# The transpose of the meta tokens' probabilities moves behind the filler products

## The chip, the core and the metric

The kernel runs on one core of a Trainium2 chip. The core has TensorE (PE, which multiplies and transposes), VectorE (DVE), ScalarE (ACT), GpSimd (POOL) and SyncE (SP, which issues most DMAs). Each engine works through its own queue in the order in which it was written; between engines semaphores say when a tile is ready or free. TensorE writes to PSUM alone, from which VectorE and ScalarE fetch. The metric is device time of one execution in microseconds (us), lower is better.

## The reference

Two layers over 1024 tokens and 16 meta tokens put ahead of them, of width 1024. A layer norms its input and projects it to Fourier features, queries, keys, values and a gate; a Fourier half and an attention half are gated and projected back. The attention has four heads, and each is the difference of two softmax maps over all 1040 positions:

```python
s = jnp.einsum('bqhcd,bkhcd->bhcqk', qb, k).astype(jnp.float32) * scale
p = jax.nn.softmax(s, axis=-1)
a = p[:, :, 0] - lam_f * p[:, :, 1]
o = jnp.einsum('bhqk,bkhd->bqhd', a, vf)
```

## The kernel before

The attention of a layer goes head by head, in four groups of two query tiles of 128 rows (in the first layer the last group has a third tile, of the 16 meta tokens). The text numbers these tiles in the order of the program: 0 to 35 in the first layer, 36 to 67 in the second. A tile goes through these steps:

- `scores`: for each of the two maps six products into the one tile S of PSUM (L633, L635; the first map is "first scores", the second "second scores"). VectorE takes S out, negated and with its row maximum, into `p` in SBUF (L640, "the maximum"), ScalarE raises it (L643). The next scores can't start before the maximum has emptied S. Of the first map's `p` there are two buffers, of the second's one. L651 mixes the two maps into the first one's `p` ("the mix").
- `drain`, one tile later: `transposes` turns the mixed map in two batches of four 128x128 transposes (L661), each into a bank M of PSUM; ScalarE and VectorE fetch each batch as a high and a low part, `ath` (L666) and `atl` (L667). The ninth transpose, L669, turns the 16 columns of the meta tokens into a third bank ("m" in the prediction); two copies (L672) and a subtraction (L673) put it into `att`.
- at the end of a group, `values`: 24 products with `ath` and `atl` (L681) and one with `att` (L682), from which `osb` is copied (L684); `finish` transposes `osb` (L695, L697) and writes the gated result.

There are three banks M, and transposes of queries (L612), of keys (L585), values and `finish` take theirs from the same three. A bank that is asked for comes free with the last fetch out of an earlier one.

Between these steps the program calls `fill(n)`: a generator hands out the projections of the next heads (L545, into banks G, with the splitting of weights into `wh` and `wl`, L180 and L181, and the norm of `qk`, L501) and then the output projection of the Fourier half (L283). These are the fillers. They have low priority and are not to be issued before the instruction that stands `LAG` entries back in `marks`, a list to which `scores` and `transposes` append.

The order of each engine's queue is not that of the program text: a scheduler lays the instructions out by priority and by its own timeline, and decides which bank and buffer each tile gets.

```python
        def drain(item, pa):
            h, gi, i, t = item
            transposes(pa, i, t)
            fill(3)
```

Of the kernel before, what the change touches and what calls it, by code (L numbers as in the profile page):

```python
# [18 lines left out]
P = 128  # L19
DEPTH = 2  # L20
D = 1024
SEQ = 1024
NMETA = 16
L = SEQ + NMETA
# [24 lines left out]
def trunk(ctx: ExitStack, tc, x, meta, ngain, w_in, w_f, qg, kg, lq1, lk1, lq2, lk2, subg, w_out,  # L49
          ident_d, chan_d, rope_d, dft_d, dftt_d, out, dbg=None):  # L50
    nc = tc.nc
    pe, act, dve, pool, sp = nc.tensor, nc.scalar, nc.vector, nc.gpsimd, nc.sync
# [12 lines left out]
    def nm(s):  # L65
        uid[0] += 1
        return f"{s}_{uid[0]}"
# [4 lines left out]
    def bank():  # L72
        return psM.tile([P, 512], F32, tag="M", name=nm("M"))
# [4 lines left out]
    def f(ap):  # L78
        return ap.bitcast(F32)


    ident = cst.tile([P, P], F32, name="ident")
# [13 lines left out]
    def tile_rows(t):  # L96
        return NMETA if t == NT else P
# [456 lines left out]
    def attention(li, wk, store, fill, marks, ready, progress):  # L554
# [13 lines left out]
        def group_tiles(gi):  # L568
            return [2 * gi, 2 * gi + 1] + ([NT] if gi == 3 and li < DEPTH - 1 else [])
# [24 lines left out]
        def build_values(h):  # L594
            va = store[h][1]
            vh = wk.tile([P, NT, P], F32R, tag="vh", name=nm("vh"), bufs=1)
            vl = wk.tile([P, NT, P], F32R, tag="vl", name=nm("vl"), bufs=1)
            act.copy(vh, va[:, 0:NT])
            pool.tensor_tensor(vl, va[:, 0:NT], f(vh), op=ALU.subtract)
            vm = va[0:NMETA, NT, :]  # L600
            for o in (0, 32, 64):
                act.copy(vt[o:o + NMETA], vm)
            pool.tensor_tensor(vt[0:NMETA], vm, f(vt[0:NMETA]), op=ALU.subtract)
            return vh, vl
# [19 lines left out]
        def scores(keys, gq, i, t, ls, gaps):  # L624
            R = tile_rows(t)
            qo = P * i
            l2 = sm.tile([P, 1], F32, tag="l2", name=nm("l2"))
            pp = []
            for c in range(2):
                q, ql, kk = gq[0][c], gq[1][c], keys[c]  # L630
                ps = big()
                for a, b in CHUNKS:
                    pe.matmul(ps[0:R, C0 + a:C0 + b], lhsT=q[:, qo:qo + R], rhs=kk[:, a:b], start=True, stop=False)  # L633
                for a, b in CHUNKS:
                    ins = pe.matmul(ps[0:R, C0 + a:C0 + b], lhsT=ql[:, qo:qo + R], rhs=kk[:, a:b],  # L635
                                    start=False, stop=True)
                marks.append(ins.ins)
                mx = sm.tile([P, 1], F32, tag=f"mx{c}", name=nm("mx"))
                pc = wk.tile([P, L], F32, tag=f"p{c}", name=nm("p"), bufs=2 - c)
                dve.tensor_scalar(pc[0:R], ps[0:R, C0:C0 + L], -1.0, None, op0=ALU.mult, op1=ALU.min,  # L640
                                  accum_out=mx[0:R])
                lc = (ls[0:R, i:i + 1], l2[0:R])[c]
                act.activation(pc[0:R], pc[0:R], AF.Exp, bias=mx[0:R], scale=-1.0, accum_out=lc)  # L643
                pp.append(pc)
                gaps[c]()
            r2 = sm.tile([P, 1], F32, tag="r2", name=nm("r2"))
            dve.reciprocal(r2[0:R], l2[0:R])
            cc = sm.tile([P, 1], F32, tag="cc", name=nm("cc"))
            dve.scalar_tensor_tensor(cc[0:R], ls[0:R, i:i + 1], lamb[0:R, li:li + 1], r2[0:R],
                                     op0=ALU.mult, op1=ALU.mult)  # L650
            dve.scalar_tensor_tensor(pp[0][0:R], pp[1][0:R], cc[0:R], pp[0][0:R], op0=ALU.mult, op1=ALU.add)  # L651
            return pp[0]

        def transposes(pa, i, t):
            R = tile_rows(t)
            qo = P * i
            for c in range(2):
                pb = bank()
                for j in range(4):
                    kt = 4 * c + j  # L660
                    pe.transpose(pb[:, R * j:R * j + R], pa[0:R, P * kt:P * kt + P],  # L661
                                 ident[0:R, 0:R])
                src = pb[:, 0:4 * R].rearrange("p (j r) -> p j r", j=4)
                hi = ath[:, 4 * c:4 * c + 4, qo:qo + R]
                with tc.high_priority(EVAC):
                    act.copy(hi, src)  # L666
                    dve.tensor_tensor(atl[:, 4 * c:4 * c + 4, qo:qo + R], src, f(hi), op=ALU.subtract)  # L667
            pb = bank()
            ins = pe.transpose(pb[0:NMETA, 0:R], pa[0:R, SEQ:L], ident[0:R, 0:R])  # L669
            marks.append(ins.ins)  # L670
            for o in (0, 64):
                act.copy(att[o:o + NMETA, qo:qo + R], pb[0:NMETA, 0:R])  # L672
            dve.tensor_tensor(att[32:32 + NMETA, qo:qo + R], pb[0:NMETA, 0:R], f(att[0:NMETA, qo:qo + R]),  # L673
                              op=ALU.subtract)

        def values(vals, w):
            vh, vl = vals
            po = bank()
            for kt in range(NT):
                for i, (v, a) in enumerate(((vh, ath), (vh, atl), (vl, ath))):  # L680
                    pe.matmul(po[:, 0:w], lhsT=v[:, kt, :], rhs=a[:, kt, 0:w], start=kt == 0 and i == 0, stop=False)  # L681
            pe.matmul(po[:, 0:w], lhsT=vt, rhs=att[:, 0:w], start=False, stop=True)  # L682
            osb = wk.tile([P, 272], F32, tag="osb", name=nm("osb"), bufs=1)
            act.copy(osb[:, 0:w], po[:, 0:w])  # L684
            return osb
# [35 lines left out]
        def flush_finish():  # L721
            if fin[0] is not None:
                finish(*fin[0])
                fin[0] = None

        def drain(item, pa):
            h, gi, i, t = item
            transposes(pa, i, t)
            fill(3)
            tiles = group_tiles(gi)  # L730
            if i == len(tiles) - 1:
                flush_finish()
                osb = values(vals[h], sum(tile_rows(t) for t in tiles))
                fin[0] = (h, gi, osb, sums[h, gi])
                if gi == 3 and h + 1 < NH:
                    vals[h + 1] = build_values(h + 1)
# [7 lines left out]
        for n, item in enumerate(items):  # L744
            h, gi, i, t = item
            if i == 0:
                sums[h, gi] = sm.tile([P, 3], F32, tag="ls", name=nm("ls"))
            pa = scores(keys[h], queries[h, gi], i, t, sums[h, gi],
                        (lambda: (fill(2), flush_finish()), lambda: fill(2)))
            if i == 0 and gi < 3:  # L750
                queries[h, gi + 1] = build_queries(h, gi + 1)
            if gi == 0 and i == 0 and h > 0:
                fill(XHD[li])
            if pend is not None:
                drain(*pend)
            if h + 1 < NH and gi >= KEYS[li]:
                build_keys(h + 1, progress.get(h + 1, 0), 1)
            pend = (item, pa)
            fill(1)
            if gi == 3 and i == len(group_tiles(3)) - 2:  # L760
                yield h + 1
                if h + 1 < NH:
                    build_keys(h + 1, 3)
                    queries[h + 1, 0] = build_queries(h + 1, 0)
        fill(3)
        drain(*pend)
        flush_finish()

# [84 lines left out]
    with tc.tile_pool(name="in0", bufs=2, side="right", reuse_waits="tile") as wk:  # L853
        for t in list(range(MT)) + [NT] + list(range(MT, NT)):
            R = tile_rows(t)
# [9 lines left out]
    for li in range(DEPTH):  # L865
# [12 lines left out]
        marks, done, ready, nh, post = [], {0}, set(), {}, {}  # L878
# [17 lines left out]
        def fill(n):  # L896
            credit[0] += n * FILL[li]
            while credit[0] >= 1.0:
                credit[0] -= 1.0
                with ExitStack() as es:  # L900
                    es.enter_context(tc.high_priority(0))
                    if len(marks) >= LAG[li]:
                        es.enter_context(tc.issue_after(marks[-LAG[li]]))
                    if next(filler, False) is False:
                        return
# [95 lines left out]
```

## Time and profile before

| | us |
|---|---|
| median of 3 runs (1213.86 to 1215.79) | 1213.92 |
| the profiled execution | 1215.41 |
| its span in the trace | 1213.6 |
| TensorE busy | 1163.2 |
| VectorE busy | 833.5 |
| ScalarE busy | 675.9 |
| GpSimd busy | 148.5 |

The span is the time from the first to the last instruction that the trace shows; the time of the execution has a little around it. A row of waits says which engine, before which line, waited for which engine's line, how long in all, how often, and the longest. In a timeline the bracket at the end of a row is the idle time of the engine just before it and what ended it. The ends of matmuls are modelled, so that rows on TensorE overlap; the distance of two starts tells what one takes.

### The profile page before, as it was taken

To read this page: it belongs to the slowest core of one execution; us is meant where nothing else is said; L and a number is where in the kernel's file an instruction comes from. 1 tells how busy PE (TensorE), PEld (TensorE's weight loads), DVE (VectorE), ACT (ScalarE), POOL (GpSimd) and SP (SyncE) were. 2 spreads that over 40 slices of the span, in tenths; PEclk is the share of its full clock that TensorE was granted. 3 is DMA by queue.
4 is the path that set the end of the run, shared out by engine and by line. 5 is a ranking of instruction groups with operands and counts; after the bars stand their busy time and mean duration, and the time that the engine had idled before them with its cause. 6 is when DMAs were issued, how large, how long until landed. Compare 5 with 4: busy or idle time off the path is not lost.

```text
span 1213.6 us, 18701 instructions
## 1 busy us (share of the span) xinstructions
PE 1163.2 (96%) x6676; PEld 1001.6 (83%) x6676; DVE 833.5 (69%) x1803; ACT 675.9 (56%) x1644; POOL 148.5 (12%) x157
## 2 busy tenths in 40 slices
PE   6999999999999999999999999999999999999998
PEld 5999986877787787788879999877888888878786
DVE  6352546788788789888683525367787887987863
ACT  5332325677767667666453223356676776866740
POOL 1101023010211201100011000140111112101000
PEclk9999999999999998999999999999999999999899
DMA  7420303012012014744335202030120210473253
GB/s 236 134 70 18 91 28 101 7 31 77 14 47 61 14 32 148 221 150 131 134 127 167 70 19 90 29 100 8 43 58 23 57 49 20 143 220 128 101 159 117
DMA packets 103613, 105.46 MB, mean 87 GB/s; under 512 B 11233, under 2 KB 87585, under 8 KB 103265
## 3 DMA queue, kind: packets, MB, share of 16 engines
q1 hardware_dynamic: 103104, 99.59, 26.4%
q0 software_dynamic: 416, 4.70, 1.1%
q8 instruction: 52, 0.85, 0.3%
q14 instruction: 41, 0.33, 0.1%
HBM read 74.62 MB, written 29.62 MB: 86 GB/s over the span
## 4 chain that ended last, share of the span: by engine, by line
PE 80%; DVE 8%; ACT 6%; DMA 3%; issue 2%; POOL 1%; SPq 1%; ACTq 0%; DVEq 0%; POOLq 0%
PE G L545 23%; PE G L283 13%; PE G L349 8%; PE S L349 7%; PE M L681 7%; PE S L633 4%; PE S L635 4%; PE M L661 3%; PE S L545 3%; DVE p L640 2%; PE M L390 2%; ACT p L643 2%; DVE p L651 1%; DMA wst<-in_w_in_dram 1%; PE M L401 1%
## 5 line engine op out<-in xcount | busy, mean ns | idle before, releaser
L545 PE MATMUL G<-wh,hT 128*128 128x512 f32 x896 | 307.5, 400 | 2.8 <-ACT va L484 1.0
L545 PEld LDWEIGHTS G<-wh,hT 128*128 128x128 f32 x896 | 167.4, 188 | 42.9 <-ACT wh L180 1.9
L643 ACT ACTIVATE p<-p,mx 128x1040 f32<-128x1040 f32 x136 | 158.6, 1166 | 69.6 <-DVE p L640 68.4
L640 DVE TENSOR_SCALAR_CACHE_REDUCE p<-S 128x1040 f32<-128x1040 f32 x136 | 167.9, 1234 | 40.7 <-PE S L635 33.4
L545 PE MATMUL G<-wl,hT 128*128 128x512 f32 x448 | 176.4, 395 | 0.6 <-DVE wl L181 0.6
L283 PE MATMUL G<-wh,yh 128*128 128x512 f32 (+2 forms) x276 | 107.4, 402 | 6.5 <-ACT yh L789 4.0
L181 DVE TENSOR_TENSOR wl<-wst,wh 128x512 fp32r<-128x512 f32 x128 | 85.7, 701 | 29.5 <-ACT wh L180 29.2
L283 PE MATMUL G<-wl,yh 128*128 128x512 f32 (+2 forms) x276 | 105.8, 392 | 0.0
L180 ACT CAST wh<-wst 128x512 fp32r<-128x512 f32 x128 | 74.7, 620 | 52.5 <-DMA wst<-in_w_in_dram 23.5
L545 PEld LDWEIGHTS G<-wl,hT 128*128 128x128 f32 x448 | 84.3, 188 | 16.3 <-DVE wl L181 1.2
L349 PE MATMUL G<-hT,wh 128*128 128x384 f32 (+3 forms) x384 | 96.4, 331 | 0.0
L283 PE MATMUL G<-wh,yl 128*128 128x512 f32 (+1 forms) x260 | 93.0, 398 | 0.0
L499 POOL TENSOR_TENSOR rsq<-ss,nhalf 128x12 f32<-128x12 f32 x24 | 54.9, 2287 | 307.0 <-DVE ss L497 261.8
L349 PE MATMUL S<-hT,wh 128*128 128x256 f32 (+3 forms) x384 | 91.0, 321 | 1.4 <-DVE sg L437 1.3
L667 DVE TENSOR_TENSOR atl<-M,ath 128x512 fp32r<-128x512 f32 x136 | 86.2, 655 | 5.5 <-ACT ath L666 4.6
L651 DVE SCALAR_TENSOR_TENSOR p<-p,cc,p 128x1040 f32<-128x1040 f32 (+1 forms) x68 | 88.2, 1297 | 1.3
L635 PE MATMUL S<-k,ql 128*128 128x264 f32 (+3 forms) x408 | 88.1, 323 | 0.0
L666 ACT CAST ath<-M 128x512 fp32r<-128x512 f32 x136 | 72.7, 565 | 15.3 <-PE M L661 14.5
L661 PE MATMUL M<-ident,p 128*128 128x128 f32 x544 | 73.8, 271 | 0.1
L681 PE MATMUL M<-ath,vh 128*128 128x256 f32 (+1 forms) x256 | 73.4, 287 | 0.2 <-DVE atl L667 0.2
L681 PE MATMUL M<-ath,vl 128*128 128x256 f32 (+1 forms) x256 | 73.0, 285 | 0.0
L681 PE MATMUL M<-atl,vh 128*128 128x256 f32 (+1 forms) x256 | 72.8, 284 | 0.0
(193 smaller groups left out, 2408.1 us busy)
## 6 DMA issues: line engine op xcount, KB each, us to landing
wst<-in_w_in_dram SPq DMA_DIRECT2D x64, 192.0 KB, 2.8
xt<-in_x_dram SPq DMA_DIRECT2D x16, 512.0 KB, 3.9
wst<-in_w_in_dram SPq DMA_DIRECT2D x32, 256.0 KB, 4.5
wst<-in_w_out_dram SPq DMA_DIRECT2D x16, 512.0 KB, 4.3
xmid<-xt SPq DMA_DIRECT2D x16, 512.0 KB, 2.8
xt<-xmid SPq DMA_DIRECT2D x16, 512.0 KB, 4.6
tab<-in_dft_dram POOLq DMA_DIRECT2D x2, 2096.0 KB, 10.9
yfd<-sg SPq DMA_DIRECT2D x8, 520.0 KB, 2.7
```

The lines of the kernel that those rows point to most:

```text
L180: act.copy(h, self.staged[q][:, j, :])
L181: dve.tensor_tensor(l, self.staged[q][:, j, :], f(h), op=ALU.subtract)
L283: pe.matmul(pb[0:m, 0:e - c], lhsT=a[:, k, 0:m], rhs=b[2 * k + n][:, c:e], start=k == 0 and i == 0, stop=k == 3 and i == n_pass - 1)
L349: pe.matmul(o, lhsT=w[k][:, c:c + P], rhs=hT[:, k, s, a:b], start=k == 0 and i == 0, stop=k == KT - 1 and i == 2)
L545: pe.matmul(pss[t][0:part.shape[-1], a:b], lhsT=part, rhs=w[k][:, a:b], start=k == 0 and i == 0, stop=k == KT - 1 and i == len(pairs) - 1)
L635: ins = pe.matmul(ps[0:R, C0 + a:C0 + b], lhsT=ql[:, qo:qo + R], rhs=kk[:, a:b], start=False, stop=True)
L640: dve.tensor_scalar(pc[0:R], ps[0:R, C0:C0 + L], -1.0, None, op0=ALU.mult, op1=ALU.min, accum_out=mx[0:R])
L643: act.activation(pc[0:R], pc[0:R], AF.Exp, bias=mx[0:R], scale=-1.0, accum_out=lc)
L651: dve.scalar_tensor_tensor(pp[0][0:R], pp[1][0:R], cc[0:R], pp[0][0:R], op0=ALU.mult, op1=ALU.add)
L661: pe.transpose(pb[:, R * j:R * j + R], pa[0:R, P * kt:P * kt + P], ident[0:R, 0:R])
L667: dve.tensor_tensor(atl[:, 4 * c:4 * c + 4, qo:qo + R], src, f(hi), op=ALU.subtract)
L681: pe.matmul(po[:, 0:w], lhsT=v[:, kt, :], rhs=a[:, kt, 0:w], start=kt == 0 and i == 0, stop=False)
```

## The change

The ninth transpose with its three followers becomes a function of its own, and `drain` calls it behind `fill(3)` instead of ahead of it. The mark that `transposes` appends is now the last of the eight transposes, no longer the ninth.

```diff
--- before.py
+++ after.py
@@ -658,16 +658,19 @@
                 pb = bank()
                 for j in range(4):
                     kt = 4 * c + j
-                    pe.transpose(pb[:, R * j:R * j + R], pa[0:R, P * kt:P * kt + P],
-                                 ident[0:R, 0:R])
+                    ins = pe.transpose(pb[:, R * j:R * j + R], pa[0:R, P * kt:P * kt + P], ident[0:R, 0:R])
                 src = pb[:, 0:4 * R].rearrange("p (j r) -> p j r", j=4)
                 hi = ath[:, 4 * c:4 * c + 4, qo:qo + R]
                 with tc.high_priority(EVAC):
                     act.copy(hi, src)
                     dve.tensor_tensor(atl[:, 4 * c:4 * c + 4, qo:qo + R], src, f(hi), op=ALU.subtract)
+            marks.append(ins.ins)
+
+        def meta_transpose(pa, i, t):
+            R = tile_rows(t)
+            qo = P * i
             pb = bank()
-            ins = pe.transpose(pb[0:NMETA, 0:R], pa[0:R, SEQ:L], ident[0:R, 0:R])
-            marks.append(ins.ins)
+            pe.transpose(pb[0:NMETA, 0:R], pa[0:R, SEQ:L], ident[0:R, 0:R])
             for o in (0, 64):
                 act.copy(att[o:o + NMETA, qo:qo + R], pb[0:NMETA, 0:R])
             dve.tensor_tensor(att[32:32 + NMETA, qo:qo + R], pb[0:NMETA, 0:R], f(att[0:NMETA, qo:qo + R]),
@@ -727,6 +730,7 @@
             h, gi, i, t = item
             transposes(pa, i, t)
             fill(3)
+            meta_transpose(pa, i, t)
             tiles = group_tiles(gi)
             if i == len(tiles) - 1:
                 flush_finish()
```

What the scheduler makes of it differs in many places from the first drain on. The first place is the drain of tile 9, on TensorE. M_3341 is the ninth transpose, S_3397 further down the second scores of tile 11. Before, from the second batch of transposes on:

```order
L661 MATMUL M_3334<-ident,p_3121 128x128 x4
L669 MATMUL M_3341<-ident,p_3121 16x128
L545 MATMUL G_3553<-wh_2816,hT_150 128x512
L545 MATMUL G_3553<-wl_2817,hT_150 128x512
L545 MATMUL G_3553<-wh_2816,hT_150 128x512
L545 MATMUL G_3553<-wh_2820,hT_150 128x512
```

Fifteen more fillers follow there, then two transposes of queries, then the scores S_3397. After, the end of the fillers and what follows:

```order
L545 MATMUL G_3553<-wl_2840,hT_150 128x512
L545 MATMUL G_3553<-wh_2839,hT_150 128x512
L673 MATMUL M_3350<-ident,p_3121 16x128
L612 MATMUL M_3419<-ident,qk_2029 128x128 x2
L661 MATMUL M_3430<-ident,p_3250 128x128 x4
L633 MATMUL S_3397<-k_2604,qb_3167 128x264
L633 MATMUL S_3397<-k_2604,qb_3167 128x512
```

The 18 fillers now stand ahead of the ninth transpose (L673 after the change), and six transposes lie between it and the scores.

The second place is VectorE's queue at tiles 57 and 58. p_11323 is written by the mix of tile 57 (L651), p_11443 by the first maximum of tile 58 (L640). Before, from the reciprocal that precedes the mix to that maximum:

```order
L647 RECIPROCAL r_2085_11389<-l_2066_11314 128x1
L649 SCALAR_TENSOR_TENSOR cc_11391<-ls_11196,lamb,r_2085_11389 128x1
L651 SCALAR_TENSOR_TENSOR p_11323<-p_11360,cc_11391,p_11323 128x1040
L667 TENSOR_TENSOR atl<-M_11394,ath 128x4x128
L501 TENSOR_TENSOR qk_10641<-qk_10641,rsq_11628 128x768
L667 TENSOR_TENSOR atl<-M_11401,ath 128x4x128
L181 TENSOR_TENSOR wl_11505<-wst_11502,wh_11504 128x512
L181 TENSOR_TENSOR wl_11509<-wst_11502,wh_11508 128x512
L512 TENSOR_TENSOR r_2135_11631<-qk_10641,cgt 128x192
L513 TENSOR_TENSOR r_2136_11632<-qk_10641,sgt 128x12x8
L514 TENSOR_TENSOR r_2136_11632<-qk_10641,sgt 128x12x8
L640 TENSOR_SCALAR p_11443,mx_11442<-S_11435 128x1040
```

After, from that maximum on, in two pieces that follow each other; first the fetches, `qk` and the keys:

```order
L640 TENSOR_SCALAR p_11443,mx_11442<-S_11435 128x1040
L181 TENSOR_TENSOR wl_11499<-wst_11492,wh_11498 128x512
L666 TENSOR_TENSOR atl<-M_11401,ath 128x4x128
L676 TENSOR_TENSOR att<-M_11417,att 16x128
L647 RECIPROCAL r_2085_11389<-l_2066_11314 128x1
L708 TENSOR_SCALAR so_11340<-so_11340 128x2
L501 TENSOR_TENSOR qk_10641<-qk_10641,rsq_11628 128x768
```

and then up to the mix:

```order
L649 SCALAR_TENSOR_TENSOR cc_11391<-ls_11196,lamb,r_2085_11389 128x1
L589 SCALAR_TENSOR_TENSOR k_11080<-M_11422,kgc,k_11080 64x384
L181 TENSOR_TENSOR wl_11505<-wst_11502,wh_11504 128x512
L711 TENSOR_TENSOR rso_11345<-rso_11345,r_2072_11338 128x2
L512 TENSOR_TENSOR r_2135_11631<-qk_10641,cgt 128x192
L513 TENSOR_TENSOR r_2136_11632<-qk_10641,sgt 128x12x8
L651 SCALAR_TENSOR_TENSOR p_11323<-p_11360,cc_11391,p_11323 128x1040
```

The mix of tile 57 stood nine instructions ahead of the maximum and now stands thirteen behind it.

The third place is TensorE's queue at the same tiles after the change. M_11401 is the second batch of transposes of tile 56, M_11417 its ninth, S_11435 and S_11452 are the first and the second scores of tile 58, M_11422 holds keys:

```order
L661 MATMUL M_11401<-ident,p_11206 128x128 x4
L673 MATMUL M_11417<-ident,p_11206 16x128
L633 MATMUL S_11435<-k_10045,qa_11250 128x264
L633 MATMUL S_11435<-k_10045,qa_11250 128x512
L633 MATMUL S_11435<-k_10045,qa_11250 128x264
L635 MATMUL S_11435<-k_10045,ql_8650 128x264
L635 MATMUL S_11435<-k_10045,ql_8650 128x512
L635 MATMUL S_11435<-k_10045,ql_8650 128x264
L585 MATMUL M_11422<-ident,qk_10641 128x128 x3
L633 MATMUL S_11452<-k_10046,qb_11251 128x264
L633 MATMUL S_11452<-k_10046,qb_11251 128x512
```

Before, 18 fillers stood between the first scores and the ninth transpose of tile 56, and six more fillers, keys and the first batch of tile 57 (p_11323) between that and the second scores; now the ninth transpose stands ahead of the first scores, and keys alone between the two scores.

## Rows read from the trace of the kernel before

**Rows 1.** The page: busy time and share of the engines, granted clock by slice
```profile
PE 1163.2 (96%) x6676; PEld 1001.6 (83%) x6676; DVE 833.5 (69%) x1803; ACT 675.9 (56%) x1644; POOL 148.5 (12%) x157
...
PEclk9999999999999998999999999999999999999899
```

**Rows 2.** Waits of TensorE from 187 to 1176 us: engine, tile, line, releaser
```profile
PE M L669 <- DVE atl L667: 13.2, 10, 1.8
PE S L633 <- DVE p L640: 5.2, 6, 1.4
PE G L283 <- ACT yh L789: 4.0, 2, 2.7
...
PE M L695 <- ACT osb L684: 0.8, 1, 0.8
...
PE M L669 <- DVE ql L620: 0.5, 2, 0.3
...
PE M L669 <- ACT osb L697: 0.2, 1, 0.2
```

**Rows 3.** Timeline at tile 9, TensorE and VectorE (start, length, what)
```profile
321.39 0.65 PE L661 MATMUL M<-ident,p 128*128 128x128 f32 x4
...
322.78 1.28 DVE L667 TENSOR_TENSOR atl<-M,ath 128x512 fp32r<-128x512 f32 x2
...
323.51 0.28 PE L669 MATMUL M<-ident,p 128*16 128x128 f32 x1 [1.48 <-DVE atl L667]
```

**Rows 4.** Timeline between the two scores of tile 37
```profile
828.60 0.39 PE L545 MATMUL G<-wl,hT 128*128 128x512 f32 x1
828.83 0.40 PE L545 MATMUL G<-wh,hT 128*128 128x512 f32 x1
...
828.57 1.24 DVE L640 TENSOR_SCALAR_CACHE_REDUCE p<-S 128x1040 f32<-128x1040 f32 x1 [0.77 <-PE S L635]
...
829.87 0.75 PE L633 MATMUL S<-k,qb 128*128 128x264 f32 x3 [0.65 <-DVE p L640]
```

**Rows 5.** Timeline where m releases a maximum, TensorE and VectorE
```profile
870.51 0.27 PE L669 MATMUL M<-ident,p 128*16 128x128 f32 x1
...
870.82 1.24 DVE L640 TENSOR_SCALAR_CACHE_REDUCE p<-S 128x1040 f32<-128x1040 f32 x1 [1.46 <-PE M L669]
```

**Rows 6.** Timeline of TensorE ahead of the second scores of tile 57
```profile
1126.89 0.38 PE L612 MATMUL M<-ident,qk 128*128 128x128 f32 x2
1127.11 0.60 PE L661 MATMUL M<-ident,p 128*128 128x128 f32 x4
1127.47 0.72 PE L633 MATMUL S<-k,qb 128*128 128x264 f32 x3
...
1128.52 0.39 PE L283 MATMUL G<-wh,yl 128*128 128x512 f32 x1
```

**Rows 7.** VectorE's groups by line: busy us, mean ns, idle before
```profile
L651 DVE SCALAR_TENSOR_TENSOR p<-p,cc,p 128x1040 f32<-128x1040 f32 (+1 forms) x68 | 88.2, 1297 | 1.3
...
L667 DVE TENSOR_TENSOR atl<-M,ath 128x512 fp32r<-128x512 f32 x136 | 86.2, 655 | 5.5 <-ACT ath L666 4.6
L181 DVE TENSOR_TENSOR wl<-wst,wh 128x512 fp32r<-128x512 f32 x128 | 85.7, 701 | 29.5 <-ACT wh L180 29.2
...
L589 DVE SCALAR_TENSOR_TENSOR k<-M,kgc,k 64x384 fp32r<-64x384 f32 (+1 forms) x48 | 27.7, 577 | 16.2 <-ACT k L588 15.1
...
L501 DVE TENSOR_TENSOR qk<-qk,rsq 128x768 f32<-128x768 f32 x24 | 23.3, 972 | 6.0 <-POOL rsq L499 5.9
```

**Rows 8.** Stretches: busy time of each engine, granted clock (PEclk), DMA
```profile
253.00:256.00 3.00, 1.19 (x8) 0.80 (x7) 2.90 (x7) 2.17 (x7) 2.27 (x1) 1.00 0.29 85
...
470.00:476.00 6.00, 5.88 (x27) 5.84 (x28) 5.90 (x16) 4.14 (x11) 0.00 (x0) 0.51 0.99 312
...
1142.00:1148.00 6.00, 5.85 (x21) 5.17 (x22) 2.56 (x6) 3.95 (x11) 0.00 (x0) 0.50 0.00 0
```

**Rows 9.** The chain that ended last: 24 value products of a group
```profile
432.70 2.83 PE M L681 x24
```

## The prediction

> **What bounds the kernel now.** I read the page first: TensorE is busy for 1163.2 of 1213.6 us [rows 1], so the time changes by what is added to or taken from its 50 us of idle time, nearly nothing else. Next came the waits of TensorE between 187 and 1176 us, the two attention stretches with the ends of their layers [rows 2]. The transpose of the meta tokens' probabilities (L669, "m" below) waits 13.2 us for the vector engine's `atl` in 10 places, 0.5 us for `ql` and 0.2 us for a copy of `osb`: 13.9 us, over a quarter of all idle time. Second are the scores (S, L633), 5.2 us behind the maximum L640 that empties their only PSUM tile.
>
> The timeline at tile 9 shows what m waits for [rows 3]: its transposes start at 321.39, the pair of `atl` at 322.78, each about 0.65, and m starts at 323.51, when the first of the pair is done. The three M banks are then held, two by the tile's own transposes, and m gets the first that is emptied. All work behind m on TensorE waits, though the filler products there need nothing of it.
>
> **The change part by part.** No instruction is added or removed, on any engine; m still brings two copies on ScalarE and a subtraction on the vector engine, and no DMA. They feed the last value product alone, and the 24 value products ahead of it, 2.83 us [rows 9], hide them. The sum is made against the profiled execution, 1215.4 us around its span of 1213.6, which is 1.5 above the median of the runs, 1213.9.
>
> *Removed.* With the filler products between the transposes and m, a bank is free when m is reached: at tile 9, 18 of them at 0.23 us [rows 4] are 4.1 us, against the 1.48 waited. I take all of the 13.9 us as gone and count apart the places where m waits anew. -13.9.
>
> *The cover that is taken from the scores.* m is the last reader of `p`, which has two buffers, so the first maximum two tiles on can't write before m is done, and the second scores of that tile can't write S before this maximum is done. A maximum released by m alone starts 0.31 after m's start [rows 5] and takes 1.24; the scores follow a maximum's end by 0.06 (828.57 + 1.24 = 829.81, scores at 829.87 [rows 4]). So 1.61 us lie from m to the second scores. Before, the filler products stood there: 18 at tile 9. After, they stand ahead of m, and behind it are two transposes of queries and four of the next tile's probabilities, which took 0.58 from 1126.89 to 1127.47 [rows 6]; with 0.1 for m itself (a transpose's slot by the same rows), 1.61 - 0.68 = 0.93 us is waited. So little stands behind m at nine tiles (7, 9, 18, 27, 44, 46, 52, 60, 62): 8.4 us. At two (2, 11) three transposes of queries stand there, 0.1 more cover: 1.7. At six (13, 15, 16, 20, 25, 54) two or three filler products remain as well, and 0.2 to 0.5 is waited: 2.3. Together +12.4. That such a wait is real, the trace before has once: at 828.83 the last of only three filler products between two scores, then 0.65 of idle time [rows 4]. Behind the maximum that waits for m stand a gate, `att`, `ql` and the next tile's `atl`, which gives M banks back; nothing on TensorE asks for those before its second scores. The lower bound is 0, if something else on TensorE is late there anyway; the upper is a further 0.5 at each of the 17, for a vector engine still busy with other work when m ends, 8 us.
>
> *Two places where the vector engine's order turns.* At tiles 57 and 58 the mix L651 of tile 57, which its transposes need, stood ahead of tile 58's first maximum; now it stands thirteen instructions behind it. Count from the end of 57's second scores. Their maximum ends 0.3 + 1.24 later, at 1.5; `atl` and `wl` (0.66 and 0.70 [rows 7]) come before 58's first maximum, which so ends at 4.1. TensorE has by then issued 58's first scores, which wait for 57's maximum themselves, to about 1.6 + 1.0, and three transposes of keys, 0.3: the second scores wait 1.2. Behind that maximum stand `wl` 0.70, `atl` 0.66, the scaling of `qk` 0.97, `k` 0.58, `wl` 0.70 and the mix 1.30 [rows 7]: ready at 9.0. TensorE has scores (1.0) and four filler products (0.9) to do from 4.1, so to 6.0, and waits 3.0. That is 4.2 without the short instructions in between; seven lie in the second part alone, and with some 0.2 each for them and their like in the first part 6.5. I take 5.5. At tiles 49 and 50 three transposes of keys are likewise all that stands between two scores, behind a maximum that two `atl` and a `wl` precede: 1.5 + 2.0 + 1.24 = 4.8, against 2.9 of work: 1.9, and 0.3 for the first scores. +5.5 and +2.2. If `exp` or a cast is later than counted, each can be 3 worse; if the casts that feed `wl` aren't late and `atl` overlaps, 0.
>
> *m waits anew* at tile 14 (second half of its transposes directly ahead of it, banks held by keys): `wl`, `k`, `atl` behind a maximum, 0.31 + 1.24 + 0.70 + 0.58 + 0.66 = 3.5, against 2.9 of work, 0.6; at tile 23 with two `wl` more, 4.9 against 3.5, 1.4. And tile 7's first scores stand only four transposes behind tile 6's last: 1.5 - 0.4 = 1.1. +3.1.
>
> *Waits of before that go.* The 0.8 for `osb` [rows 2] is covered, since ten filler products now stand ahead of it; of the 5.2 behind maxima I take 1.9 as gone, a third, between 0 and all but the 0.65 that stays. -2.7. Of the 2.7 for `yh` at 1142, where the copy stood behind a weight cast, that cast now stands behind the copy, but ahead of `osb`: bound 0 and -2.7, I take -1.4.
>
> Fillers left after the last tile fall from 132 to 104: 28 x 0.23 = 6.4 us of products that now run earlier. That is no gain on a queue that is never empty. The mark that the fillers are held by is now the last probabilities' transpose instead of m, seven or eight marks back: nothing.
>
> Sum: -13.9 - 2.7 - 1.4 + 12.4 + 7.7 + 3.1 = +5.2. From 1215.4 that is 1220.6, and by the median 1.5 less: **1219**.
>
> **The clock.** At 253 to 256 us m's longest wait leaves the granted clock at 1.00, the full 2.4 GHz; after the 2.7 us of idle time for `yh` it is 0.50, 1.2 GHz, for the six us from 1142, which costs 3 us, and the same stands at 470 to 476 [rows 8], behind waits around tile 23. So a long wait can cost as much again. The Trainium skill (TensorE: Matmul & The Clock Gate, section "A second HAM failure mode: psum-queue depth-cycling") says that short idle stretches from cycling through PSUM banks make the clock swing; by that, taking away thirteen bank waits would give clock back, at most the 3 us of one of the two stretches. The trace agrees little: behind m's longest wait the clock stays up, and no slice of the page is below 8 tenths of it [rows 1].
>
> **Rivals.** (1) *Faster*: the bank waits go and the vector engine's turned order costs nothing, since the mixes come in time as before. Then 7.7 is out of the sum and the 17 places cost a third less, 8: 1215.4 - 18.0 + 8 + 3.1 - 1.5 = 1207. For it speaks that the vector engine is busy for 69% only; against it that its order is fixed and that the mix stands behind `k` and `wl`. It decides from the point where tile 57's transposes find their mix within 1.9 us of 58's second scores. (2) *The wait only changes its place*: 13.9 us at m become 12 to 16 at the scores, all else cancels: 1212 to 1216. (3) *Slower by the clock*: the 4 to 7 us at tiles 57 and 58, or the two waits at tile 23, are followed by half clock as at 1142; 3 us each, and with the 8 us of the upper bound at the 17 places: 1222 to 1234. (4) *Clock comes back*: the weights' wait near 1142 shrinks enough that the clock stays up there, 1219 - 3 = 1216; that the wait for `osb` takes its place speaks against it. The skill's rule named above would lead here too.
>
> **How the numbers follow.** Forecast, 1216 to 1222: 0.39. Rival 3: 0.17. Rival 2 with 4: 0.22. Rival 1, 1203 to 1211: 0.22. A measurement of this kernel tells about 0.2%, 2.4 us, from no change; forecast and rival 3 are slower but for 0.02, rival 1 faster. So faster 0.22, same 0.24, slower 0.54. Leaving out about 0.1 at each end, the range is 1207 to 1229; the forecast's own is 1216 to 1222.
>
> **What would show it.** m's idle time falls from 13.9 to about 2. S behind L640 rises from 5.2 to about 16, in some 20 waits near 0.9. Tile 57's transposes wait 2 us or more for L651. If S behind L640 stays under 8 us, the cover step is wrong; if tile 57 doesn't wait, the order step is; if m still waits 10 us, the first is. DVE and ACT busy time stay.

## The result, and the profile after

The changed kernel takes 1229.35 us (median of four runs, 1227.64 to 1232.7) against 1214.13 for the kernel before, measured beside it: a ratio of 1.013, 95% interval 1.0111 to 1.0148. The direction was forecast; the size was not, +15 us where +5 stood, and the time lies 0.35 us above the range. One run of the kernel before that belongs to the experiments below took 2307.52 us, in the slow state, and is left out of every ratio and mean.

The profiled execution took 1228.29 us, 12.9 more than that of before; both had a mean granted clock of 0.994. From the page, busy time of the engines and TensorE's clock by slice:

```profile
PE 1166.3 (95%) x6676; PEld 999.1 (81%) x6676; DVE 837.8 (68%) x1803; ACT 675.4 (55%) x1644; POOL 153.6 (13%) x157
...
PEclk9999999999999999999999999999999999899999
```

Against [rows 1] TensorE is busy for 3.1 us more and idle for 9.8 more (1226.5 - 1166.3 = 60.2, where it was 50.4). VectorE is busy for 4.3 us more, with the same number of instructions, ScalarE for 0.5 less. The waits of TensorE from 187 to 1190 us (releaser: total us, times, longest) answer to [rows 2]:

```profile
PE S L633 <- DVE p L640: 20.7, 24, 1.8
PE M L673 <- DVE atl L666: 3.2, 2, 2.2
PE G L283 <- ACT yh L256: 2.1, 1, 2.1
PE G L283 <- ACT yh L793: 1.7, 2, 1.0
...
PE M L698 <- ACT osb L687: 1.5, 2, 1.0
PE S L633 <- DVE so L708: 1.4, 2, 0.7
...
PE M L661 <- ACT osb L700: 1.1, 1, 1.1
PE M L661 <- DVE p L651: 1.0, 2, 0.6
...
PE M L673 <- ACT osb L700: 0.4, 1, 0.4
```

m (now L673) waits 3.6 us instead of 13.9. The scores wait 22.1 behind the maximum instead of 5.2: 20.7, and 1.4 at two places where the row names `so`, a short instruction that follows the maximum on VectorE and ends just after it. At tile 9, the place of [rows 3], the timeline of TensorE and then the maximum on VectorE read:

```profile
320.76 0.38 PE L661 MATMUL M<-ident,p 128*128 128x128 f32 x2
320.90 0.48 PE L545 MATMUL G<-wh,hT 128*128 128x512 f32 x1
...
325.18 0.27 PE L673 MATMUL M<-ident,p 128*16 128x128 f32 x1
325.29 0.38 PE L612 MATMUL M<-ident,qk 128*128 128x128 f32 x2
325.50 0.60 PE L661 MATMUL M<-ident,p 128*128 128x128 f32 x4
326.79 0.74 PE L633 MATMUL S<-k,qb 128*128 128x264 f32 x3 [0.69 <-DVE so L708]
...
325.49 1.24 DVE L640 TENSOR_SCALAR_CACHE_REDUCE p<-S 128x1040 f32<-128x1040 f32 x1 [0.63 <-PE M L673]
```

The filler products start right behind the transposes, m finds its bank free, the maximum starts 0.31 us after m, and the second scores 1.61 us after m. This is the forecast's chain, with its numbers. At 15 of the 17 places it named, such a wait stands, 11.8 us together (forecast 12.4).

But the maximum starts these 0.31 us after m at only seven of the 17 places. At the other ten it starts 0.39 to 1.85 us after m, right behind other work on VectorE. So the sum fits better than its parts: the nine places of 0.93 us wait from 0 to 1.30. At tile 60:

```profile
1118.76 0.27 PE L673 MATMUL M<-ident,p 128*16 128x128 f32 x1
...
1121.37 0.75 PE L633 MATMUL S<-k,qb 128*128 128x264 f32 x3 [1.17 <-DVE p L640]
...
1118.20 1.29 DVE L666 TENSOR_TENSOR atl<-M,ath 128x512 fp32r<-128x512 f32 x2 [1.63 <-ACT ath L665]
1119.41 0.68 DVE L290 TENSOR_TENSOR xt<-xt,G 128x512 f32<-128x512 f32 x1
...
1120.08 1.23 DVE L640 TENSOR_SCALAR_CACHE_REDUCE p<-S 128x1040 f32<-128x1040 f32 x1
```

m is done early enough for a maximum at 1119.07; `atl` and a residual stand ahead of it in the queue, and it starts at 1120.08. Around tiles 57 and 58 the forecast 5.5 us of waits are 4.7 (0.28, 1.85, 2.11 and 0.45). The longest is a filler's, for the cast of `yh` on ScalarE; the transposes of tile 57 wait only 0.45 for their mix. Half the clock is granted from the third wait on. TensorE, then a window (PEclk follows POOL's numbers):

```profile
1061.79 0.75 PE L633 MATMUL S<-k,qa 128*128 128x264 f32 x3 [0.28 <-DVE p L640]
...
1065.19 0.74 PE L633 MATMUL S<-k,qb 128*128 128x264 f32 x3 [1.85 <-DVE p L640]
...
1068.52 0.79 PE L283 MATMUL G<-wh,yh 128*128 128x512 f32 x1 [2.11 <-ACT yh L256]
...
1071.04 1.97 PE L661 MATMUL M<-ident,p 128*128 128x128 f32 x8 [0.45 <-DVE p L651]
...
1067.00:1074.00 7.00, 5.03 (x16) 3.88 (x16) 6.90 (x15) 4.88 (x9) 1.33 (x1) 0.51 0.63 204
```

### The profile page after: what moved, and what is told of

It is laid out like the page before. It is cut to its first block, busy times and chain, and to the rows that moved or that the text cites. A ratio compares the mean times of both kernels' runs of the same rounds, so it can differ in the third digit from the quotient of the medians.

```text
span 1226.5 us, 18693 instructions
## 1 busy us (share of the span) xinstructions
PE 1166.3 (95%) x6676; PEld 999.1 (81%) x6676; DVE 837.8 (68%) x1803; ACT 675.4 (55%) x1644; POOL 153.6 (13%) x157
## 4 chain that ended last, share of the span: by engine, by line
PE 72%; DVE 10%; ACT 6%; issue 5%; DMA 4%; POOL 1%; SPq 1%; DVEq 0%; POOLq 0%; ACTq 0%
PE G L545 22%; PE G L283 10%; PE G L349 7%; PE M L684 7%; PE S L349 6%; PE S L633 4%; PE S L635 4%; PE S L545 3%; PE M L661 3%; DVE p L640 2%; DMA wst<-in_w_in_dram 2%; PE M L390 2%; ACT p L643 1%; DVE atl L666 1%; DVE p L651 1%
## 5 line engine op out<-in xcount | busy, mean ns | idle before, releaser
L640 DVE TENSOR_SCALAR_CACHE_REDUCE p<-S 128x1040 f32<-128x1040 f32 x136 | 167.9, 1234 | 22.0 <-PE S L635 18.9
L651 DVE SCALAR_TENSOR_TENSOR p<-p,cc,p 128x1040 f32<-128x1040 f32 (+1 forms) x68 | 88.9, 1307 | 1.8
L710 POOL TENSOR_TENSOR rso<-so,nhalf 128x2 f32<-128x2 f32 (+1 forms) x36 | 31.5, 875 | 404.7 <-DVE so L708 404.7
L661 PE MATMUL M<-ident,p 128*128 128x128 f32 x544 | 76.7, 272 | 2.7 <-ACT osb L700 1.1
L661 PEld LDWEIGHTS M<-ident,p 128*128 128x128 f32 x544 | 62.6, 141 | 12.3 <-ACT osb L700 1.5
```

The source lines that it names most:

```text
L661: ins = pe.transpose(pb[:, R * j:R * j + R], pa[0:R, P * kt:P * kt + P], ident[0:R, 0:R])
```

## The experiments

Theory 1 is the forecast's: a wait for a bank ahead of m, exchanged for the cover that the fillers behind m gave the maximum that m releases. Theory 2: any change of this order costs some 10 us. Theory 3: it is the mark, not m's place in the text. Theory 4, beside 1: half-clock stretches carry a part. Each ratio is against runs of the kernel before that were measured beside it.

### What moves m

`e1_mark_only`: m stays ahead of `fill(3)`, the mark alone moves.

```diff
             transposes(pa, i, t)
-            fill(3)
             meta_transpose(pa, i, t)
+            fill(3)
```

> The meta tokens' transpose stays ahead of the filler products, as before; only the mark that holds the fillers moves to the last probabilities' transpose, which is what the change does to the marks. If the time comes from the buffers of p that the late transpose holds (theory 1): as before, 1214 within 3 us, m's waits for a bank still near 13 us and the scores' waits for a maximum near 5. If the moved mark lets fillers and their weights come at other times and this is what costs (theory 3): 1225 to 1230, with the scores' waits near 20 us.

1231.98 us, 1.0152 (1.0116 to 1.0188). Its waits, whole span:

```profile
PE S L633 <- DVE p L640: 19.4, 23, 1.9
...
PE M L673 <- DVE atl L666: 3.2, 2, 2.2
```

These are the waits of the changed kernel, within 1.3 us. The two orders of instructions, laid side by side, differ in 22 rows on TensorE and in none on the other engines. So with the mark moved, where m stands in the text decides nothing; the mark alone brings the whole change. Fillers wait for a mark, and while m was the mark, the next fillers could not go ahead of it. With the last probabilities' transpose as the mark they are free as soon as that stands in the queue, and are laid out while m has no bank.

`e2_late_marked`: the other half, m behind `fill(3)` and still the mark.

```diff
-            marks.append(ins.ins)
...
-            pe.transpose(pb[0:NMETA, 0:R], pa[0:R, SEQ:L], ident[0:R, 0:R])
+            ins = pe.transpose(pb[0:NMETA, 0:R], pa[0:R, SEQ:L], ident[0:R, 0:R])
+            marks.append(ins.ins)
```

> The changed kernel with the mark back on the meta tokens' transpose, which stands behind the three fillers. Theory 1 (the late last reader of p): as the changed kernel, 1229 within 3 us, scores' waits near 20 us, m's near 4. Theory 3 (the mark): back near 1214.

1225.8 us, 1.0088 (1.0062 to 1.0115), between the two expectations. In its order no filler product stands between the transposes and m at 31 of 68 tiles, against 41 before and 12 in the changed kernel (310 such products over all tiles, against 203 and 598); and the three fillers count back from a list that m is not yet on, so they hang on an older mark. Its scores wait 6.0 us for the maximum and m 9.8 (6.4 for `atl`, 3.4 for `ql`): neither of theory 1's prices, and still 11 us. So the place in the text does count while m is the mark. Theory 2 is not refuted here: this order, too, fits worse than that of before, by waits spread over many lines.

### Whether p's buffers are the chain

`e3_late_own_tile` and its control `e4_early_own_tile`: the mix writes the meta tokens' columns into a tile of their own, so m no longer holds `p`. The diff leaves out the calls that pass the tile on, and a buffer made smaller for room (the expectation names it).

```diff
-            dve.scalar_tensor_tensor(pp[0][0:R], pp[1][0:R], cc[0:R], pp[0][0:R], op0=ALU.mult, op1=ALU.add)
-            return pp[0]
+            dve.scalar_tensor_tensor(pp[0][0:R, 0:SEQ], pp[1][0:R, 0:SEQ], cc[0:R], pp[0][0:R, 0:SEQ],
+                                     op0=ALU.mult, op1=ALU.add)
+            pmt = sm.tile([P, NMETA], F32, tag="pmt", name=nm("pmt"))
+            dve.scalar_tensor_tensor(pmt[0:R], pp[1][0:R, SEQ:L], cc[0:R], pp[0][0:R, SEQ:L],
+                                     op0=ALU.mult, op1=ALU.add)
+            return pp[0], pmt
```

> The changed kernel, but the mix writes the 16 columns of the meta tokens into a small tile of their own (one more short instruction on the vector engine for each tile, three buffers), so the late transpose no longer holds p. To make room, the output of the squares, which nobody reads, is bfloat16. Theory 1: the waits at the 17 places where a maximum waits for m go, 11.8 us of 20.7 at the scores, while m's waits stay near 4: 1229 - 12 = 1217, and if the longer waits around tiles 49, 57 and 23 go too, down to 1207. Theory 2 (the turned order on the vector engine and ScalarE is what costs, not p): 1225 or more, scores' waits still over 15 us.

> Control for the run before: the kernel before with the same small tile and the same extra instruction on the vector engine, the transpose ahead of the fillers as before and marked. Theory 1 and 2: as before, 1214 within 4 us, m still waiting 10 to 15 us for banks; above that, the extra instruction itself costs, and the run before is to be read against this one.

1227.06 us, 1.0102 (1.0082 to 1.0121), and 1228.94 us, 1.0121 (1.0092 to 1.0151). The first has theory 1's waits and theory 2's time; the control misses its 1214. The waits of the first, then of the control:

```profile
PE S L633 <- DVE p L640: 6.7, 11, 0.9
PE S L633 <- ACT qa L619: 5.1, 4, 1.7
PE M L702 <- ACT osb L691: 4.5, 7, 1.6
PE G L794 <- DMA ya<-yad: 4.3, 1, 4.3
```

```profile
PE S L633 <- DVE p L640: 11.7, 11, 2.0
...
PE M L676 <- DVE atl L670: 6.7, 6, 1.6
PE G L794 <- DMA ya<-yad: 4.3, 1, 4.3
```

With `p` let go early the late m brings the scores' waits behind the maximum from 20.7 us down to 6.7, as the chain asks (1.4 of that has only changed its releaser's name, and those for queries, `qa`, rose from 1.6 to 5.1). Of the 17 places of the forecast only two still wait in the trace, behind the m of tiles 44 and 46, 0.53 and 0.79 us. But the extra instruction turns the order by itself: the control, with m early and marked, is 14 us above the kernel before, and both wait 4.3 us for a reload at the end of the first layer, where neither kernel of the comparison waits for one. Against each other the two are equal within their intervals, though not at one clock: their runs show 0.9905 and 0.9958 on average. The pages of the two profiles, at 0.990 and 0.997:

```profile
PE 1170.7 (96%) x6676; PEld 1003.0 (82%) x6676; DVE 845.2 (69%) x1871; ACT 675.9 (55%) x1644; POOL 155.3 (13%) x157
PE 1163.3 (95%) x6676; PEld 997.6 (81%) x6676; DVE 841.6 (69%) x1871; ACT 676.7 (55%) x1644; POOL 148.7 (12%) x157
```

With spans of 1224.8 and 1226.7 us TensorE is idle for 54.1 us with the late m and for 63.4 with the early one; 7.4 us of more busy time, at the lower clock, take most of that back. So the chain is confirmed as a wait, and as a price in time it is not isolated.

### How much cover, and in which layer

Six kernels with the code order of `e1_mark_only`, in which the first k filler units (three products each) that a mark holds hang on the last transpose and the others on m; k is given for the two layers, and k = 99 is the change. The diff shows k = 2, 0 and leaves out the lines that fill `held` and `metas`.

```diff
-                        es.enter_context(tc.issue_after(marks[-LAG[li]]))
+                        mark = marks[-LAG[li]]
+                        if id(mark) in metas:
+                            held[id(mark)] += 1
+                            mark = metas[id(mark)] if held[id(mark)] > (2, 0)[li] else mark
+                        es.enter_context(tc.issue_after(mark))
```

`q10_one_unit_layer0` (1, 0):

> As the run before with one unit (three products, 0.7 us) between the transposes and m in layer 0. Theory 1: about half of the bank waits go, 1209 to 1211, and no wait at the scores is added. Theory 2: 1216 to 1226, unlike in its details to the run with two.

`q20_two_units_layer0` (2, 0):

> Layer 1 as before. In layer 0, of the filler units that the transposes' mark held back, the first two (six products, 1.4 us) are let go by the last probabilities' transpose and the rest by m, so six products stand between the transposes and m at most tiles, and the other twelve behind m as before. Theory 1 (two prices: a bank wait ahead of m, and the cover taken from the maximum that m releases): the bank waits of layer 0, 10.3 us, shrink to about 2 and twelve products, 2.8 us, still cover the 1.61 from m to the second scores: 1214 - 8 = 1206, from 1203 to 1209. Theory 2 (any change of this order costs some 10 us elsewhere, by turned queues on the vector engine and ScalarE): 1216 to 1226.

`q30_three_units_layer0` (3, 0):

> Layer 1 as before; in layer 0 three units (nine products, 2.1 us) are let go by the last probabilities' transpose and the rest by m. Theory 1: nine products are left behind m at most tiles, 2.1 us and more than the 1.61 from m to the second scores, at some only three: bank waits of layer 0 under 2 us, scores' waits of layer 0 between the 3.9 of two units and the 9.1 of all, time between 1210 and 1215. Theory 2: 1218 and more, as with all units.

`q90_change_layer0_only` (99, 0):

> The change's order in layer 0 (all units let go by the last probabilities' transpose), layer 1 in the order of before. Idle time of the changed kernel in layer 0's attention was 1.1 us above before: 1214 + 1 = 1215, within 3 us, if the two layers' parts add up. If the cost is the fillers that layer 0 uses up earlier (theory 3), 1220 or more.

`q09_change_layer1_only` (0, 99):

> The change's marks in layer 1 only, layer 0 in the order of before. Idle time of the changed kernel in layer 1's attention was 6.3 us above before, and 1.6 in the tail, with some 2 to 3 of matmul time that stands with the breaks: 1214 + 10 = 1224, from 1221 to 1227. Less than 1219 would say that the two layers' parts do not add up.

`q21_both_layers` (2, 1):

> Two units in layer 0, as in the run with two there, and one of the two units in layer 1. Theory 1: layer 1 has only 3.4 us of bank waits to give, and with one unit fewer behind m half of the scores' waits of the changed layer 1 come: 1212 + 3 to 1212 + 6, so 1215 to 1218.

| k in layers 0, 1 | us | ratio, 95% interval | S behind L640 / m behind `atl`, first layer, without tile 0 |
|---|---|---|---|
| 0, 0 (before; 1213.26 beside 3, 0 and 2, 1) | 1213.39 | 1 | 1.3 / 10.3 |
| 1, 0 | 1211.86 | 0.9985 (0.9973 to 0.9997) | 3.2 / 5.4 |
| 2, 0 | 1211.99 | 0.9981 (0.9966 to 0.9995) | 3.9 / 3.6 |
| 3, 0 | 1216.10 | 1.0017 (1.0007 to 1.0028) | 5.9 / 0.3 |
| 99, 0 | 1218.40 | 1.0040 (1.0027 to 1.0054) | 7.8 / 3.2 |
| 0, 99 | 1224.06 | 1.0091 (1.0075 to 1.0108) | 1.3 / 10.3 |
| 2, 1 | 1216.51 | 1.0026 (1.0013 to 1.0040) | 3.9 / 3.6 |

The last column is the wait list from 215 to 590 us (tile 0's wait of 1.4 falls into it with 1, 0 and 99, 0 and is taken off). The layers add up: +0.4% and +0.9%, 16 us, against the 15 of both; so two thirds of the price lie in the second layer, where m waited for banks only 3.4 us before. The times of 0, 99 and 2, 1 lie in their expected ranges, the other four 0.4 to 3 us above them. Theory 2, that any change of the order costs some 10 us, falls with the first layer's four kernels. In the first layer the dose has the shape that theory 1 gives it: a little of the batch ahead of m pays, all of it costs, and the turn lies between two units and three. Yet two units bring 1.4 us in the median and not the 8 forecast. The wait list of that kernel from 215 to 590 us, and its tile 9:

```profile
PE S L633 <- DVE p L640: 3.9, 2, 2.3
PE M L674 <- DVE atl L666: 3.6, 4, 1.1
PE M L686 <- DVE atl L666: 0.9, 2, 0.5
...
321.15 0.28 PE L674 MATMUL M<-ident,p 128*16 128x128 f32 x1 [1.13 <-DVE atl L666]
```

6.7 us of bank waits are gone and 2.6 have come at the scores, though not at the places of theory 1. All 3.9 stand ahead of the first scores of tiles 16 and 25, and no second scores wait between 215 and 590 us:

```profile
368.96 0.74 PE L633 MATMUL S<-k,qa 128*128 128x264 f32 x3 [1.63 <-DVE p L640]
...
463.85 1.05 PE L633 MATMUL S<-k,qa 128*128 128x264 f32 x3 [2.26 <-DVE p L640]
```

With one unit it is the same two tiles (and tile 25 waited 1.3 before). So the cover held, as theory 1 says, and part of the gain went to waits that theory 1 doesn't have. The profile with two units, at a clock of 0.997, took 1208.82 us, 6.6 below that of before, which stood at 0.994: 4.2 less of idle time, the rest less busy time, at the higher clock. Over its ten runs the mean clock is 0.9959, over those of before beside them 0.9979, so over the runs the clock gave part of the gain back. The kernels with one and two units are the only ones that beat both; by 0.2%, hardly more than can be measured.

### The clock, and the cover at the end

`c_after_again` is the changed kernel once more. In `y3_tail_cover` the left-over products can't be used up ahead of the last tile:

```diff
-        run(filler)
+        with ExitStack() as es:
+            if last:
+                es.enter_context(tc.issue_after(marks[-3]))
+            run(filler)
```

> The changed kernel again, for more pairs of time and mean granted clock. If half-clock stretches carry a part of the cost (theory 4, beside theory 1), its runs lie at clocks of 0.990 to 0.996 against 0.996 to 1.000 of the kernel before, and at one clock, 0.996, the two differ by 10 to 12 us and not by 15. If the clock has no part, the times don't follow the clock.

> The changed kernel, where the products left over after layer 1's attention stand behind the second scores of the last tile, so that 164 of them remain behind the last probabilities' transpose, as in the kernel before (136 in the changed one); up to the last tile the order is that of the changed kernel. If the used-up cover costs what the traces say, the wait for the reload of ya (2.2 us) and what follows it go: 1229 - 3 = 1226. If those products were no cover, 1229.

1228.6 us, 1.0125 (1.0104 to 1.0146), and 1228.51 us, 1.0116 (1.0099 to 1.0134).

Ten runs of the changed kernel show a mean granted clock of 0.990 to 0.997, 0.9928 on average; the 62 runs of before that came with these experiments 0.993 to 1.000, 0.9973 on average. In both the time follows it: before, 1212.7 us at 0.999 (17 runs) and 1216.8 at 0.994 (5); after, 1227.4 at 0.994 (4) and 1232.5 at 0.990 (3). At the same 0.994 the difference is 10.6 us, as theory 4 expected, so of the 15.2 some 4.6 go with the clock, if its loss is taken as a cost of its own. The two profiles don't show this, since the profiled execution of before was one of its low ones. The two profiles of the changed kernel, first on record and then again, from 974 to 978 us:

```profile
974.00:978.00 4.00, 3.16 (x9) 2.69 (x10) 3.87 (x13) 3.93 (x12) 0.41 (x1) 0.61 0.29 55
```

```profile
974.00:978.00 4.00, 3.63 (x17) 3.03 (x18) 3.87 (x13) 3.90 (x13) 0.00 (x0) 1.00 0.38 96
```

The second scores of tile 50 are the last to wait ahead of it, again in the first and then in the other:

```profile
974.84 1.22 PE L633 MATMUL S<-k,qb 128*128 128x264 f32 x3 [1.69 <-DVE p L640]
```

```profile
974.37 0.74 PE L633 MATMUL S<-k,qb 128*128 128x264 f32 x3 [1.68 <-DVE p L640]
```

The first scores had waited 1.25 us in both. One execution falls to half clock here and the other doesn't.

The tail's cover is no price. From 1170 us on the changed kernel waits as in the first row, the one with its cover back as in the second:

```profile
PE G L789 <- DMA ya<-yad: 2.2, 2, 1.9
```

```profile
PE G L283 <- DVE xt L290: 2.1, 4, 1.0
```

The wait for the reload is gone, one for the residual stands in its place, and the time is the same within 2 us. The expectation of 1226 fell.

### The turned order on VectorE

`w57_mix_first` puts the mix of tile 57 back ahead of tile 58's first maximum; `w49_57_mix_first` does the same at tiles 49 and 50 too (14 beside 22). The diff leaves out the line that fills `mixes`.

```diff
+                with ExitStack() as es:
+                    if li == 1 and len(mixes) == 22:
+                        es.enter_context(tc.issue_after(mixes[-1]))
-                dve.tensor_scalar(pc[0:R], ps[0:R, C0:C0 + L], -1.0, None, op0=ALU.mult, op1=ALU.min,
+                    dve.tensor_scalar(pc[0:R], ps[0:R, C0:C0 + L], -1.0, None, op0=ALU.mult, op1=ALU.min,
```

> The changed kernel, where the vector engine's first maximum of tile 58 is queued behind the mix of tile 57, as it stood in the kernel before; nothing else is asked for, and up to that place the order is that of the changed kernel. If the turned order costs what the forecast and the trace say (4.7 us of waits between 1061 and 1071, and behind them the half-clock stretch at 1064 to 1067 that takes 3.4 us of full speed): waits there near 1, no stretch, 1229 - 4 to 1229 - 7, so 1222 to 1225. If another wait (the cast of yh on ScalarE) takes its place: 1227 to 1230.

> The same at both places, tile 50's first maximum behind the mix of tile 49 as well (3.3 us of waits there and, in two of four profiles of this order, a stretch of 1.7 us). If both places cost as forecast: 1219 to 1223. If neither: 1227 to 1230.

1227.34 us, 1.0103 (1.0082 to 1.0124), and 1229.92 us, 1.0122 (1.0100 to 1.0143). Both lie in the ranges for the case that the turned order is not the price. The first moved the wait's place alone; TensorE there, and the busy time of all engines around it, then that of the kernel before at its tiles 57 and 58:

```profile
1065.57 0.75 PE L633 MATMUL S<-k,qa 128*128 128x264 f32 x3 [0.28 <-DVE p L643]
...
1071.59 1.94 PE L664 MATMUL M<-ident,p 128*128 128x128 f32 x8 [4.47 <-DVE so L711]
...
1062.00:1071.00 9.00, 4.84 (x36) 4.04 (x34) 7.33 (x17) 8.22 (x24) 2.58 (x1) 1.00 0.83 284
1071.00:1075.00 4.00, 3.41 (x14) 3.16 (x15) 3.94 (x8) 3.05 (x6) 0.69 (x1) 0.57 0.82 263
```

```profile
1054.00:1064.00 10.00, 8.97 (x47) 6.68 (x46) 9.38 (x19) 9.08 (x22) 2.58 (x1) 1.00 0.82 279
```

The mix is ahead of the maximum now, and the transposes of tile 57 wait 4.47 us for it (the row names `so`, which stands right behind it), where the waits were 4.7; half clock follows as well, 0.57 from 1071 to 1075. ScalarE, busy for 8.22 of 9 us, much of it with casts of weights, comes to tile 57's second exponential late. In the kernel before it was as full (9.08 of 10), and VectorE too (9.38), and TensorE had products to do. In `w49_57_mix_first` the waits are 4.2 us around tiles 49 and 50 and 4.4 around 57 and 58, 2.75 and 3.19 of it for `va` and `yh` of ScalarE. So the turned order is where the wait shows and not why it is there: in this stretch ScalarE has little slack, and TensorE comes to it with fewer products that need nothing of it. That last part is argued; no run adds such products there.

## Why the prediction was right in direction and wrong in size

- **Removed, -13.9.** Nearly right, with the 2.0 counted apart for m anew (-11.9 net): measured -10.3. m waits 2.23 us at tile 23 (1.4 forecast) and 1.01 at tile 14 (0.6); tile 7's first scores wait 1.43 (1.1).
- **Cover taken from the scores, +12.4.** Right as a sum, 11.8 at 15 of 17 places, with some luck in it: at ten places the maximum comes later than m releases it. All waits behind the maximum rose by 16.9 us.
- **Tiles 57/58 and 49/50, +5.5 and +2.2.** Near in size, 4.7 and 3.3 (0.35 of it m's), and in part not for the reason given. The second scores wait behind the maximum as reasoned, 1.85 and 1.69 (1.2 and 1.9 forecast). But of the 3.0 for tile 57's mix, whose sign was a wait of 2 us or more, 0.45 came, with 2.11 for `yh` ahead of it; with the mix put back in its order the wait moved.
- **Waits that go, -2.7 and -1.4.** The second is right (-1.5). The first failed: the 0.8 for `osb` didn't go, 2.6 came (L698, and L661 behind a copy of `osb`), and of the six waits behind a maximum of before all six still stand.
- **Fillers used up early: no gain.** A new wait of 2.2 us stood in the tail, but giving the cover back changed no time.
- **The mark: "nothing".** Wrong as a mechanism, and without effect on the sum, which was worked out from the orders themselves: the moved mark brings the whole change, as `e1_mark_only` shows.
- **No price beyond idle time.** The forecast starts from TensorE's idle time and "nearly nothing else". But TensorE is also busy for 3.1 us more, at the same clock of 0.994. The breaks may have a price of their own: at tile 9 of [rows 3] m starts 2.12 us after the first of its four transposes, where the next instruction starts 0.36 after four such in [rows 6]; 1.48 of the 1.76 between is booked as idle, the rest, 0.28, as busy. From 187 us on the timeline holds 56 breaks where it held 38; at 0.28 each, 18 more would be 5 us, an estimate from one place. Profiles at 0.997 agree in direction only: 1160.9 us busy with two units (36 breaks), 1163.3 in `e4_early_own_tile` (52), 1163.6 in the changed kernel again (56). What makes the busy time was not isolated.
- **Clock: no term in the sum.** Wrong. From 0.9973 to 0.9928 on average, 4.6 us of the difference.

Profile against profile, at one clock, +5.2 were forecast and +12.9 measured: 9.8 of idle time, 3.1 of busy time. Between the medians the clock adds the rest, 2.3 by these two profiles and 4.6 by the averages at 0.994.

So the step that failed is the first one, that the time moves with TensorE's idle time alone: 3.1 us of busy time and the 2.3 to 4.6 of the clock stood at nothing in the sum, the clock although rival 3 priced it. Within the idle time the term for waits that go failed: -2.7 was forecast, `osb` alone went from 0.8 to 2.6, and the waits behind maxima stayed. Rival 3's mechanism, half clock at tiles 57 and 58, did come, and the measured time lies in its range of 1222 to 1234. Yet the changed kernel's profile has no more loss by the clock than that of before, and the rival's other part, 8 us for a busy VectorE at the 17 places, didn't come. Rivals 1 and 4 didn't come; rival 2's wait at the scores did, its time didn't.

What stays open: why `e2_late_marked` costs 11 us, with m behind fillers at fewer tiles than in the changed kernel, and `e4_early_own_tile`, whose m is early, 14. They show that some orders near that of before fit this program worse, while one and two units fit it as well; which places decide was not taken apart.

## What to carry to other kernels

Where a scheduler lays out the queues, look for what its ordering edges hang on before believing that a line's place in the text moves it. A bank wait covered by filler work is paid for where that filler stood before: follow the last reader of each buffer to the wait that it releases. Moving a part of the filler paid 0.2% here, in one layer, and moving all of it cost. Where TensorE is busy for 96%, compare profiles and runs at the same granted clock, and compare busy time as well as idle time.

## What was not expected of the hardware

The same instructions with the same waits directly ahead, within 0.01 us, were followed by half clock in one execution and by full clock in another (974 to 978 us, above). Over the 62 runs of the kernel before the mean clock of a run lies between 0.993 and 1.000, and its time between 1210.8 and 1219.1 us.

The Trainium skill (TensorE: Matmul & The Clock Gate, section "A second HAM failure mode: psum-queue depth-cycling") says that short idle stretches from cycling through PSUM banks make the clock swing. From that the prediction drew, with doubt, that the clock would come back with fewer bank waits. It didn't: m's waits fell from 13.9 to 3.6 us and the mean clock fell too. This is no test of what the Trainium skill says, as other waits came in their place; in the changed kernel's profile the half-clock stretches stand behind the long waits around tiles 23, 49 and 57, and the first of these places had one before [rows 8].
